# Q and K of a block in one input buffer, Q in the even partitions and K in the odd ones

## The chip, the cores and the metric

The kernel runs on one core of one Trainium2 chip. The metric is the device time of one execution in microseconds (us), median of several runs. A core has five engines that run side by side: TensorE (PE, matrix products), VectorE (DVE), ScalarE (ACT), GpSimd (POOL) and SyncE (SP). Sixteen DMA engines move data between the chip's memory (HBM) and the on-chip memory SBUF, which has 128 partitions. SP and ACT issue the transfers of this kernel, each through a queue of its own; the profile calls SP's data queue q1 and ACT's q10.

## The reference

```python
batch, n_heads, seq, head_dim = 8, 12, 1024, 64
def reference(q, k):
    return np.einsum('bhid,bhjd->bhij', q, k).astype(np.float32)
```

Each of the 8 x 12 = 96 heads is a product of a 1024 x 64 matrix Q with the transpose of a 1024 x 64 matrix K. Inputs and output are float32. The inputs are 2 x 25.2 MB, the output 402.7 MB.

## The kernel before

The 96 heads are worked in 11 blocks of 2, 2, 4, 8, 8 and then six times 12 heads (`sizes`). For each head, PE forms eight row tiles of 128 x 1024 scores (`scores`, L256): for each tile a weight load of Q (L317) and two products with 512 columns of K (L320), with a contraction over 64 partitions. ACT copies the scores from PSUM into one of three output buffers `o_sb` (L289), two tiles at a time, four copies per head; in the very first head DVE takes every second tile. After the last copy of a head, SP stores the whole buffer of 4 MB as one transfer (L305). A head may only be copied into an `o_sb` buffer when the store from three heads before has landed.

PE needs Q and K transposed (head_dim on partitions) and in half precision. For blocks 0 and 1 PE transposes (L244). For blocks 2 to 10 the way is:

- **Load** (L152 to L163). One transfer each for Q and K of the block brings the block's rows into 128 partitions, each partition a contiguous run of `R * D` floats with R = N * 1024 / 128 (24 KB for 12 heads). Q and K take turns in a ring of two buffers `x_sb`, so in practice one of them holds Q and the other K. Blocks 0 to 2 are loaded at the start into an output buffer that is still free, block 3 at the start into `x_sb`; all of these are SP's (and for single heads of K, ACT's). From block 4 on, ACT issues the loads, between its copies: `LOADS` (L81) tells after the second copy of which heads of block i the next load in the stream is issued; where no entry stands, it is heads 6 and 8. ACT waits there until all casts from that buffer are done.
- **Cast** (L201 to L220). POOL casts a chunk to half precision, four instructions of 32 partitions each, which also place the pieces for the transpose. A block of 12 heads has four chunks of 128 x 3072: Q in two parts, K in two parts. There are two buffers `half_sb` for them; block 2's chunks lie in unused ends of the operand buffers (`rooms`).
- **Transpose** (L222 to L236). DVE transposes a chunk in 32 x 32 squares into the operand buffers `qk_sb`, of which there are two sets, used by even and odd blocks. The first transpose of block i therefore waits until PE has finished block i - 2 (`over`).

Every engine works through its own list in order; the lists wait for one another only through counters. The transposes are written out beside the heads of the block before (`side` in `block`, L400), but DVE has nothing else to do after the start, so it runs them as soon as their casts and `over` allow. POOL, too, has only its list of casts.

Of the kernel before, what the change touches and what calls it, by code (L numbers as in the profile page):

```python
# [6 lines left out]
F16 = mybir.dt.float16  # L7
F32 = mybir.dt.float32
P = 128
# [50 lines left out]
def kernel(  # L60
# [6 lines left out]
    nc = tc.nc  # L67

    B, H, S, D = q.shape
# [8 lines left out]
    PE_BLOCKS, EARLY = 2, 3  # L78
    NMAX = max(sizes)
    CHUNK, HALVES = 96 * 32, 2  # L80
    LOADS = {0: (), 1: (), 2: (1, 3), 3: (4, 6), 4: (4, 6)}  # L81

    pool = ctx.enter_context(tc.tile_pool(name="sb", bufs=1))
    psum = ctx.enter_context(
        tc.tile_pool(name="ps", bufs=1, space=bass.MemoryType.PSUM)
    )
    ident = pool.tile([P, P], F16, tag="ident")
    x_sb = [pool.tile([P, NMAX * S * D // P], F32, name=f"x_sb{i}", tag=f"x{i}") for i in range(2)]
    half_sb = [pool.tile([P, CHUNK], F16, name=f"half{i}", tag=f"half{i}") for i in range(HALVES)]
    qk_sb = [  # L90
        [pool.tile([P, NMAX * S // 2], F16, name=f"{'qk'[x]}T{i}") for x in range(2)]
        for i in range(2)
    ]
    o_sb = [pool.tile([P, NT, S], F32, name=f"o_sb{i}", tag=f"out{i}") for i in range(3)]
# [10 lines left out]
    class Ring:  # L105
# [9 lines left out]
        def next(self):  # L115
# [4 lines left out]

    halves = Ring(half_sb)
    n, at = S * D // P * 2, 8 * S // 2
    rooms = Ring(
        [
            qk_sb[i][x][:, at + h * n : at + (h + 1) * n]
            for i in (1, 0)
            for x in range(2)
            for h in range(2)
        ]
    )  # L130
    inputs = Ring(x_sb)
    outs = Ring(o_sb)
    input_landing = {id(t): Landing(nc, f"x{i}_in") for i, t in enumerate(x_sb)}
    store_landing = {id(t): Landing(nc, f"out{i}_out") for i, t in enumerate(o_sb)}

    class Block:
        def __init__(self, i, first, N):
            self.i, self.first, self.N = i, first, N
            self.by_pe = i < PE_BLOCKS
            self.R = N * S // P  # L140
            self.elems = self.R * D
            self.cut = max(1, -(-self.R * 32 // CHUNK))
            self.raw = [None] * 2
            self.landed = [[] for _ in range(2)]
            self.raw_busy = [None] * 2
            self.rows = [None] * 2
            self.halves = {}
            self.qk = qk_sb[i % 2]
            self.ready = []
            self.over = []  # L150

        def load(self, x, eng, landing=None):  # L152
            events = []
            if self.raw[x] is None:
                buf, events, self.raw_busy[x] = inputs.next()
                self.raw[x] = buf[:, : self.elems]
                landing = input_landing[id(buf)]
            src = flat[x][self.first * S : (self.first + self.N) * S]
            eng.wait(events)
            dma = eng.eng.dma_start(  # L160
                out=self.raw[x], in_=src.rearrange("(p r) d -> p (r d)", p=P)
            )
            self.landed[x].append(landing.start(dma))  # L163

        def load_head(self, n, x, eng, landing):
            start = (self.first + n) * S
            m = S * D // P
            dma = eng.eng.dma_start(  # L168
                out=self.raw[x][:, n * m : (n + 1) * m],
                in_=flat[x][start : start + S].rearrange("(p r) d -> p (r d)", p=P),  # L170
            )
            self.landed[x].append(landing.start(dma))

        def cast_rows(self, x):
            n = S * D // P
            buf, events, busy = rooms.next()
            rows = buf[:, : 2 * n].rearrange("p (r h d) -> p r h d", h=2, d=D)
            for h in range(2):
                done = gps.run(
                    lambda: nc.gpsimd.tensor_copy(  # L180
                        out=rows[:, :, h],
                        in_=self.raw[x][:, h * n : (h + 1) * n].rearrange(
                            "p (r d) -> p r d", d=D
                        ),
                    ),
                    events + [self.landed[x][h]],
                )
            self.rows[x] = rows, done, busy
            if self.raw_busy[x] is not None:
                self.raw_busy[x].append(done)  # L190
            return done

        def chunks(self):
            return [
                (x, part, c)
                for x in range(2)
                for part in range(2)
                for c in range(self.cut)
            ]

        def cast_quads(self, x, part, c):  # L201
            m = self.R // self.cut
            buf, events, busy = (rooms if self.i == PE_BLOCKS else halves).next()
            dst = buf[:, : m * 32]
            raw = self.raw[x].rearrange("p (r h d) -> p r h d", h=2, d=32)
            for half in range(2):
                b = 2 * half + part
                for h in range(2):
                    q0 = 32 * (2 * half + h)
                    done = gps.run(  # L210
                        lambda: nc.gpsimd.tensor_copy(  # L211
                            out=dst[q0 : q0 + 32].rearrange("p (r d) -> p r d", d=32),
                            in_=raw[32 * b : 32 * b + 32, c * m : (c + 1) * m, h],
                        ),
                        events + self.landed[x],
                    )
            self.halves[x, part, c] = dst, done, busy
            if self.raw_busy[x] is not None:
                self.raw_busy[x][:] = [done]
            return done  # L220

        def transpose_quads(self, x, part, c):  # L222
            buf, cast, busy = self.halves.pop((x, part, c))
            n, m = self.N * S // 4, self.R // self.cut
            dst = self.qk[x][:, part * n : (part + 1) * n].rearrange(
                "c (i r) -> c r i", i=32
            )[:, c * m : (c + 1) * m]
            before = blocks[self.i - 2].over if self.i >= 2 else []
            done = dve.run(
                lambda: nc.vector.transpose(  # L230
                    out=dst, in_=buf.rearrange("p (r i) -> p r i", i=32)
                ),
                [cast] + before,
            )
            busy.append(done)
            self.ready.append(done)  # L236
# [103 lines left out]
    raw = early.rearrange("p t j -> p (t j)")  # L340
    at = 0
    for b in blocks[:EARLY]:
        for x in range(2):
            b.raw[x] = raw[:, at : at + b.elems]
            at += b.elems
        if b.by_pe:
            for n in range(b.N):
                for x in range(2):
                    b.load_head(n, x, (sp, act)[x], Landing(nc, f"e{b.i}{n}{x}"))
        else:  # L350
            for x in range(2):
                b.load(x, sp, Landing(nc, f"e{b.i}{x}"))
# [6 lines left out]
    def next_load(eng):  # L359
        if stream:  # L360
            b, x = stream.pop(0)
            assert b.i == EARLY or not any(i == b.i - 1 and c[0] == x for i, c in casts)
            b.load(x, eng)

    for x in range(2):
# [18 lines left out]
    def to_half(last):  # L384
        while casts:
            i, c = casts[0]
            if i > last or (blocks[i], c[0]) in stream:
                return
            if not (rooms if i == PE_BLOCKS else halves).free():
                return  # L390
            done = blocks[i].cast_quads(*c)
            if i == 2:
                early_busy[:] = [done]
            casts.pop(0)
# [5 lines left out]
    def block(i, heads, regions, w):  # L400
        b = blocks[i]
        nxt = blocks[i + 1] if i + 1 < len(blocks) else None
        for n in heads:
            side = {}
            if nxt and nxt.by_pe:
                if n == 1:
                    side = {
                        u: [
                            lambda x=u // 2: nxt.transpose_rows(
                                x, regions.next(), dve, nc.vector.tensor_copy  # L410
                            )
                        ]
                        for u in (1, 3)
                    }
            elif nxt:
                parts = nxt.chunks()
                some = [s for m, s in enumerate(parts) if m * b.N // len(parts) == n]
                side = {0: [lambda s=s: transposed(nxt, s) for s in some]}
            if n in LOADS.get(i, (6, 8)):
                side[1] = side.get(1, []) + [lambda: next_load(act)]  # L420
            b.scores(n, side, regions, w)
            to_half(i + 2 + (n == b.N - 1))
# [50 lines left out]
```

## Time and profile before

| what | value |
|---|---|
| median of 3 runs | 1062.28 us (1061.65 to 1062.32) |
| profiled execution | 1061.94 us |
| its span, first to last instruction | 1059.8 us |
| PE, ACT, DVE, POOL busy | 66%, 66%, 44%, 33% |
| moved by DMA | 453.19 MB, mean 428 GB/s |
| read from HBM, written to HBM | 50.33 MB, 402.65 MB |

The page of the profile has, for each engine, the time in which it executed instructions, the span in 40 equal slices (a digit is tenths of busy time; for DMA the mean over the 16 engines, and the GB/s that they moved), the DMA queues with packets and bytes and the share of the 16 engines' time that their packets took, a chain of work followed back from the last instruction, and groups of equal instructions by line. In a group, "x96 | 263.3, 2743 | 466.9 <-DMA ..." means 96 instructions, 263.3 us in total, 2743 ns each, and 466.9 us of idle time of that engine ahead of them, with what ended the idle time. For transfers the last number is the median time from issue to landing. A row of the view of waits names who waited, for whom, the total in us, how often and the longest wait. In the view of windows, a row gives a stretch of the span, its length, the busy time of PE, PE's weight loads, DVE, ACT and POOL with their instruction counts, the clock, the DMA share and the GB/s.

### The profile page before, as it was taken

What the parts mean: (1) busy time and instruction counts of PE and PEld (TensorE: products, weight loads), DVE (VectorE), ACT (ScalarE), POOL (GpSimd) and SP (SyncE); (2) the same over time, 40 slices, a digit from 0 to 9 for tenths busy, and PEclk for the clock granted to TensorE, in tenths of its full rate; (3) what the DMA queues carried; (4) which work ended last, traced back from release to release, by engine and by line L of the source; (5) the groups of instructions that cost most, each with busy time, mean ns of one, the idle gap of its engine ahead of it and who ended that gap; (6) DMA issues with size and microseconds to landing.
All of it is one profiled execution on the core that took longest, in us unless ns stands there. A gap on an engine that the chain in (4) does not pass through costs nothing.

```text
span 1059.8 us, 3258 instructions
## 1 busy us (share of the span) xinstructions
PE 700.6 (66%) x1568; PEld 127.2 (12%) x800; DVE 470.5 (44%) x43; ACT 697.5 (66%) x386; POOL 345.7 (33%) x158
## 2 busy tenths in 40 slices
PE   6875855675577557875577755778557777778770
PEld 2111100110011001110011100111001111111110
DVE  2998701991696006970069600696007960000000
ACT  4766755665677557785577755777557778777771
POOL 7667316445370340803407043070431700000000
DMA  9999999999999999999999999999999999999998
GB/s 391 433 432 420 436 423 424 435 427 426 435 430 430 427 431 433 433 425 427 433 435 434 423 424 433 432 434 425 426 433 432 434 435 432 434 434 429 433 433 357
DMA packets 17584, 453.19 MB, mean 428 GB/s; under 512 B 1953, under 2 KB 1953, under 8 KB 2977
## 3 DMA queue, kind: packets, MB, share of 16 engines
q1 hardware_dynamic: 14976, 410.00, 90.0%
q10 hardware_dynamic: 2592, 42.99, 9.7%
q8 instruction: 9, 0.15, 0.0%
q14 instruction: 7, 0.05, 0.0%
HBM read 50.33 MB, written 402.65 MB: 427 GB/s over the span
## 4 chain that ended last, share of the span: by engine, by line
DMA 71%; ACT 17%; PE 7%; DVE 1%; issue 1%; POOL 0%; ACTq 0%; SPq 0%
DMA out_dram<-o_sb 70%; ACT o_sb L289 17%; PE ps_all L320 7%; DVE qT L230 1%; DVE kT L230 0%; DMA o_sb<-in_q_dram 0%; PE ps_all L244 0%; POOL qT L180 0%; DVE kT L251 0%; ACT kT L251 0%; ACTq L36 0%; SPq L168 0%; SPq L468 0%; SPq L97 0%
## 5 line engine op out<-in xcount | busy, mean ns | idle before, releaser
L289 ACT COPY o_sb<-ps_all 128x2048 f32<-128x2048 f32 (+1 forms) x384 | 695.2, 1861 | 332.1 <-DMA out_dram<-o_sb 298.8
L320 PE MATMUL ps_all<-kT,qT 64*128 64x512 f16 x1536 | 696.5, 616 | 327.2 <-ACT o_sb L289 321.8
L211 POOL CAST half<-x_sb 32x3072 f16<-32x3072 f32 (+1 forms) x128 | 323.7, 2529 | 491.4 <-DMA x_sb<-in_q_dram 245.9
L230 DVE STREAM_TRANSPOSE qT<-half 128x3072 f16<-128x3072 f16 (+1 forms) x16 | 222.8, 14127 | 370.7 <-PE ps_all L320 368.9
L317 PEld LDWEIGHTS <-qT 64*128 64x128 f16 x768 | 124.1, 162 | 896.5 <-issue 889.0
L230 DVE STREAM_TRANSPOSE kT<-half 128x3072 f16<-128x3072 f16 (+1 forms) x16 | 224.2, 14219 | 3.4 <-POOL half L211 3.4
L230 DVE STREAM_TRANSPOSE kT<-kT 128x1024 f16<-128x1024 f16 x2 | 9.4, 4873 | 0.0
L230 DVE STREAM_TRANSPOSE qT<-qT 128x1024 f16<-128x1024 f16 x2 | 9.2, 4786 | 0.0
L211 POOL CAST qT<-o_sb 32x1024 f16<-32x1024 f32 x8 | 8.3, 1036 | 1.2 <-DMA o_sb<-in_q_dram 0.8
L211 POOL CAST kT<-o_sb 32x1024 f16<-32x1024 f32 x8 | 8.3, 1036 | 0.5
L251 DVE COPY qT<-ps_all 128x1024 f16<-128x1024 f16 x2 | 2.4, 1224 | 10.8 <-PE ps_all L244 10.8
L289 DVE COPY o_sb<-ps_all 128x1024 f32<-128x1024 f32 x4 | 4.9, 1225 | 4.4 <-PE ps_all L320 4.4
L244 PE MATMUL ps_all<-ident,qT 128*128 128x128 f16 x16 | 2.1, 311 | 6.5 <-POOL qT L180 6.4
L251 ACT COPY kT<-ps_all 128x1024 f16<-128x1024 f16 x1 | 1.0, 1013 | 4.6 <-PE ps_all L244 4.6
L180 POOL CAST qT<-o_sb 128x512 f16<-128x512 f32 x4 | 2.3, 613 | 3.5 <-DMA o_sb<-in_q_dram 3.5
L251 DVE COPY kT<-ps_all 128x1024 f16<-128x1024 f16 x1 | 1.2, 1225 | 4.3 <-PE ps_all L244 4.3
L251 ACT ACT_TABLE_LOAD x1 | 1.3, 1283 | 2.8 <-issue 2.8
L180 POOL CAST kT<-o_sb 128x512 f16<-128x512 f32 x4 | 2.3, 614 | 1.3 <-DMA o_sb<-in_q_dram 1.3
L244 PE MATMUL ps_all<-ident,kT 128*128 128x128 f16 x16 | 2.0, 306 | 0.7 <-ACT o_sb L289 0.7
L244 PEld LDWEIGHTS ps_all<-ident,qT 128*128 128x128 f16 x16 | 1.5, 141 | 6.8 <-POOL qT L180 6.8
L244 PEld LDWEIGHTS ps_all<-ident,kT 128*128 128x128 f16 x16 | 1.5, 138 | 3.3 <-POOL qT L211 1.6
L372 POOL TENSOR_SCALAR_AFFINE_SELECT ident<-ident 128x128 f16<-128x128 f16 x1 | 0.3, 295 | 0.2 <-POOL ident L368 0.2
(5 smaller groups left out, 0.6 us busy)
## 6 DMA issues: line engine op xcount, KB each, us to landing
out_dram<-o_sb SPq DMA_DIRECT2D x96, 4096.0 KB, 21.5
x_sb<-in_q_dram ACTq DMA_DIRECT2D x6, 3072.0 KB, 22.7
x_sb<-in_k_dram ACTq DMA_DIRECT2D x6, 3072.0 KB, 22.0
x_sb<-in_q_dram SPq DMA_DIRECT2D x1, 2048.0 KB, 15.5
x_sb<-in_k_dram SPq DMA_DIRECT2D x1, 2048.0 KB, 20.9
x_sb<-in_q_dram ACTq DMA_DIRECT2D x1, 2048.0 KB, 19.2
x_sb<-in_k_dram ACTq DMA_DIRECT2D x1, 2048.0 KB, 20.2
o_sb<-in_k_dram ACTq DMA_DIRECT2D x4, 256.0 KB, 4.9
```

The costliest lines, as they stand in the source:

```text
L180: lambda: nc.gpsimd.tensor_copy(out=rows[:, :, h], in_=self.raw[x][:, h * n : (h + 1) * n].rearrange("p (r d) -> p r d", d=D),),
L211: lambda: nc.gpsimd.tensor_copy(out=dst[q0 : q0 + 32].rearrange("p (r d) -> p r d", d=32), in_=raw[32 * b : 32 * b + 32, c * m : (c + 1) * ...
L230: lambda: nc.vector.transpose(out=dst, in_=buf.rearrange("p (r i) -> p r i", i=32)),
L244: lambda: nc.tensor.transpose(t_ps[:, t], rows[:, t], ident),
L251: lambda: copy(out=dst, in_=t_ps.rearrange("c t m -> c m t")), [done]
L289: lambda: (nc.vector.tensor_copy if by_dve else nc.scalar.copy)(out=dst, in_=ps[:, : w * S]),
L317: return nc.tensor.ldweights(stationary, tile_position=(at, 0))
L320: return nc.tensor.add_instruction(mybir.InstMatmult(name=nc.get_next_instruction_name(), ins=[nc.tensor.lower_ap(moving), nc.tensor.lower ...
L372: lambda: nc.gpsimd.affine_select(out=ident, in_=ident, compare_op=mybir.AluOpType.not_equal, fill=1.0, base=0, pattern=[[-1, P]], channel ...
```

## The change

There is now one input buffer `x_sb` of 128 partitions and twice the length, as much memory as the two before. A block's rows of Q are cut into 64 runs instead of 128, each twice as long (48 KB for 12 heads), which go to partitions 0, 2, 4, ...; those of K go to partitions 1, 3, 5, ... Each load is still one transfer, now with 64 partitions in steps of two. This holds for blocks 2 to 10; the loads of single heads for blocks 0 and 1 keep their form.

A chunk for POOL and DVE then has Q and K together. A block of 12 heads still has four chunks of 128 x 3072 (`chunks`: two parts by two cuts), 8-head blocks four of 128 x 2048, and block 2 two of 128 x 2048 instead of four of 128 x 1024. The casts wait for both loads of the block. The transpose writes to Q's and K's operand buffer by turns, since they are now two halves of one tile, 12288 bytes apart.

Since Q and K share the buffer, a load of the next block waits until all casts of the block before are done, and `LOADS` is set anew: block 4's loads are issued in head 3 of block 2 and head 0 of block 3, block 5's in heads 6 and 7 of block 3, block 6's in head 7 of block 4 and head 0 of block 5, block 7's in heads 8 and 10 of block 5, and those of blocks 8 to 10 in heads 6 and 8 of the block two before. The transposes of the next block are written out beside heads 1 to N - 1 instead of 0 to N - 1. The buffers for block 2's chunks and for blocks 0 and 1 are two separate rings.

```diff
-    LOADS = {0: (), 1: (), 2: (1, 3), 3: (4, 6), 4: (4, 6)}
+    LOADS = {0: (), 1: (), 2: (3,), 3: (0, 6, 7), 4: (7,), 5: (0, 8, 10)}
...
-    x_sb = [pool.tile([P, NMAX * S * D // P], F32, name=f"x_sb{i}", tag=f"x{i}") for i in range(2)]
+    x_sb = pool.tile([P, NMAX * S * D // (P // 2)], F32, tag="x")
...
-        [pool.tile([P, NMAX * S // 2], F16, name=f"{'qk'[x]}T{i}") for x in range(2)]
+        pool.tile([P, 2, NMAX * S // 2], F16, name=f"qkT{i}", tag=f"qkT{i}")
...
-            self.R = N * S // P
+            self.R = N * S // (P // 2)
...
-            eng.wait(events)
+            eng.wait(self.free)
             dma = eng.eng.dma_start(
-                out=self.raw[x], in_=src.rearrange("(p r) d -> p (r d)", p=P)
-            )
-            self.landed[x].append(landing.start(dma))
+                out=self.raw[x::2], in_=src.rearrange("(a r) d -> a (r d)", a=P // 2)
+            )
+            self.landed[x].append((landing or input_landing[x]).start(dma))
...
         def chunks(self):
-            return [
-                (x, part, c)
-                for x in range(2)
-                for part in range(2)
-                for c in range(self.cut)
-            ]
+            return [(part, c) for part in range(2) for c in range(self.cut)]
...
-                        events + self.landed[x],
+                        events + self.landed[0] + self.landed[1],
...
-            n, m = self.N * S // 4, self.R // self.cut
-            dst = self.qk[x][:, part * n : (part + 1) * n].rearrange(
-                "c (i r) -> c r i", i=32
-            )[:, c * m : (c + 1) * m]
+            n, m = self.N * S // 2, self.R // self.cut
+            dst = qk_sb[self.i % 2][:, :, :n].rearrange(
+                "c x (t a r) -> c t r a x", t=2, r=self.R
+            )[:, part, c * m : (c + 1) * m]
             before = blocks[self.i - 2].over if self.i >= 2 else []
             done = dve.run(
                 lambda: nc.vector.transpose(
-                    out=dst, in_=buf.rearrange("p (r i) -> p r i", i=32)
+                    out=dst, in_=buf.rearrange("p (r a x) -> p r a x", a=16, x=2)
                 ),
...
-                some = [s for m, s in enumerate(parts) if m * b.N // len(parts) == n]
+                some = [s for m, s in enumerate(parts) if 1 + m * (b.N - 1) // len(parts) == n]
```

More of the change, by code (lines that the diff above doesn't have):

```diff
@@ L122 @@
     n, at = S * D // P * 2, 8 * S // 2
[L123 to L126, printed above, removed]
-            for x in range(2)
-            for h in range(2)
-        ]
-    )
-    inputs = Ring(x_sb)
+    unused = [[qk_sb[i][:, x, at:] for x in range(2)] for i in range(2)]
+    row_rooms = Ring([r[:, h * n : (h + 1) * n] for r in unused[1] for h in range(2)])
+    rooms = Ring(unused[0])
+    inputs = Ring([x_sb])
     outs = Ring(o_sb)
-    input_landing = {id(t): Landing(nc, f"x{i}_in") for i, t in enumerate(x_sb)}
+    input_landing = [Landing(nc, f"x{x}_in") for x in range(2)]
     store_landing = {id(t): Landing(nc, f"out{i}_out") for i, t in enumerate(o_sb)}
@@ L139, in __init__ @@
             self.by_pe = i < PE_BLOCKS
-            self.R = N * S // P
+            self.R = N * S // (P // 2)
             self.elems = self.R * D
             self.cut = max(1, -(-self.R * 32 // CHUNK))
-            self.raw = [None] * 2
+            self.raw = None
+            self.free = []
             self.landed = [[] for _ in range(2)]
-            self.raw_busy = [None] * 2
+            self.raw_busy = None
             self.rows = [None] * 2
             self.halves = {}
-            self.qk = qk_sb[i % 2]
+            self.qk = [qk_sb[i % 2][:, x] for x in range(2)]
             self.ready = []
@@ L152, in load @@
         def load(self, x, eng, landing=None):
[L153 to L157, printed above, removed]
+            if self.raw is None:
+                buf, self.free, self.raw_busy = inputs.next()
+                self.raw = buf[:, : self.elems]
             src = flat[x][self.first * S : (self.first + self.N) * S]
-            eng.wait(events)
+            eng.wait(self.free)
             dma = eng.eng.dma_start(
-                out=self.raw[x], in_=src.rearrange("(p r) d -> p (r d)", p=P)
+                out=self.raw[x::2], in_=src.rearrange("(a r) d -> a (r d)", a=P // 2)
             )
-            self.landed[x].append(landing.start(dma))
+            self.landed[x].append((landing or input_landing[x]).start(dma))
         def load_head(self, n, x, eng, landing):
@@ L168, in load_head @@
             dma = eng.eng.dma_start(
-                out=self.raw[x][:, n * m : (n + 1) * m],
+                out=self.raw[:, (x * self.N + n) * m : (x * self.N + n + 1) * m],
                 in_=flat[x][start : start + S].rearrange("(p r) d -> p (r d)", p=P),
@@ L175, in cast_rows @@
             n = S * D // P
-            buf, events, busy = rooms.next()
+            buf, events, busy = row_rooms.next()
             rows = buf[:, : 2 * n].rearrange("p (r h d) -> p r h d", h=2, d=D)
@@ L181, in cast_rows @@
                         out=rows[:, :, h],
-                        in_=self.raw[x][:, h * n : (h + 1) * n].rearrange(
-                            "p (r d) -> p r d", d=D
-                        ),
+                        in_=self.raw[
+                            :, (x * self.N + h) * n : (x * self.N + h + 1) * n
+                        ].rearrange("p (r d) -> p r d", d=D),
                     ),
@@ L188, in cast_rows, with cast_quads @@
             self.rows[x] = rows, done, busy
-            if self.raw_busy[x] is not None:
-                self.raw_busy[x].append(done)
             return done
         def chunks(self):
-            return [
-                (x, part, c)
-                for x in range(2)
-                for part in range(2)
-                for c in range(self.cut)
-            ]
-        def cast_quads(self, x, part, c):
+            return [(part, c) for part in range(2) for c in range(self.cut)]
+        def cast_quads(self, part, c):
             m = self.R // self.cut
@@ L204, in cast_quads @@
             dst = buf[:, : m * 32]
-            raw = self.raw[x].rearrange("p (r h d) -> p r h d", h=2, d=32)
+            raw = self.raw.rearrange("p (r h d) -> p r h d", h=2, d=32)
             for half in range(2):
@@ L214, in cast_quads, with transpose_quads @@
                         ),
-                        events + self.landed[x],
+                        events + self.landed[0] + self.landed[1],
                     )
-            self.halves[x, part, c] = dst, done, busy
-            if self.raw_busy[x] is not None:
-                self.raw_busy[x][:] = [done]
-            return done
-        def transpose_quads(self, x, part, c):
-            buf, cast, busy = self.halves.pop((x, part, c))
-            n, m = self.N * S // 4, self.R // self.cut
-            dst = self.qk[x][:, part * n : (part + 1) * n].rearrange(
-                "c (i r) -> c r i", i=32
-            )[:, c * m : (c + 1) * m]
+            self.halves[part, c] = dst, done, busy
+            if self.raw_busy is not None:
+                self.raw_busy[:] = [done]
+            return done
+        def transpose_quads(self, part, c):
+            buf, cast, busy = self.halves.pop((part, c))
+            n, m = self.N * S // 2, self.R // self.cut
+            dst = qk_sb[self.i % 2][:, :, :n].rearrange(
+                "c x (t a r) -> c t r a x", t=2, r=self.R
+            )[:, part, c * m : (c + 1) * m]
             before = blocks[self.i - 2].over if self.i >= 2 else []
@@ L342 @@
     for b in blocks[:EARLY]:
-        for x in range(2):
-            b.raw[x] = raw[:, at : at + b.elems]
-            at += b.elems
+        b.raw = raw[:, at : at + b.elems]
+        at += b.elems
         if b.by_pe:
@@ L361, in next_load @@
             b, x = stream.pop(0)
-            assert b.i == EARLY or not any(i == b.i - 1 and c[0] == x for i, c in casts)
+            assert b.i == EARLY or not any(i == b.i - 1 for i, c in casts)
             b.load(x, eng)
@@ L386, in to_half @@
             i, c = casts[0]
-            if i > last or (blocks[i], c[0]) in stream:
+            if i > last or any((blocks[i], x) in stream for x in range(2)):
                 return
```

## The prediction

> **What bounds the kernel now.** The first view is the page: the busy slices and the DMA rate, then the queues.
>
> ```profile
> span 1059.8 us, 3258 instructions
> ...
> DMA  9999999999999999999999999999999999999998
> GB/s 391 433 432 420 436 423 424 435 427 426 435 430 430 427 431 433 433 425 427 433 435 434 423 424 433 432 434 425 426 433 432 434 435 432 434 434 429 433 433 357
> DMA packets 17584, 453.19 MB, mean 428 GB/s; under 512 B 1953, under 2 KB 1953, under 8 KB 2977
> ...
> q1 hardware_dynamic: 14976, 410.00, 90.0%
> q10 hardware_dynamic: 2592, 42.99, 9.7%
> ```
>
> The DMA row is full from the first slice to the last, and the two data queues together take 90.0 + 9.7 = 99.7% of the 16 engines' time. No compute engine is above 66%. So the bytes set the time: 453.19 MB, at no slice above 436 GB/s. Nothing on PE, ACT, DVE or POOL costs anything until it makes the store queue run dry. The change moves the same bytes, so what it does to the time is what it does to the rate of the loads, unless it makes a block's operands late.
>
> The second view is the chain that ended last and the waits; the third, the landing times.
>
> ```profile
> DMA 71%; ACT 17%; PE 7%; DVE 1%; issue 1%; POOL 0%; ACTq 0%; SPq 0%
> ```
> ```profile
> DVE qT L230 <- PE ps_all L320: 368.9, 6, 72.7
> PE ps_all L320 <- ACT o_sb L289: 321.8, 187, 8.0
> ACT o_sb L289 <- DMA out_dram<-o_sb: 298.8, 88, 8.0
> ```
> ```profile
> out_dram<-o_sb SPq DMA_DIRECT2D x96, 4096.0 KB, 21.5
> x_sb<-in_q_dram ACTq DMA_DIRECT2D x6, 3072.0 KB, 22.7
> x_sb<-in_k_dram ACTq DMA_DIRECT2D x6, 3072.0 KB, 22.0
> ```
>
> ACT waits for a store to land before 88 of 96 heads, PE waits for ACT, DVE waits for PE: everyone waits for the stores. A store of 4.19 MB is about 9.7 us of DMA work (4.19 MB / 433 GB/s), and lands 21.5 us after its issue: its own 9.7, about 9.7 of the store ahead of it, and some 2 of latency. So when a store is issued one whole store still lies ahead of it: a head may come about 9.7 us late before the DMA engines idle.
>
> **The loads.** Count packets: 96 stores, 8 loads of single heads, 4 loads by SP and 14 by ACT are 122 transfers; 122 x 128 rows + 122 x 16 = 17568, which is 14976 + 2592. So one row is one packet, each transfer has 16 more small ones, one for each engine, and all transfers are now spread over 16 engines with 8 rows each. 18 loads change form (blocks 2 to 10, Q and K): 64 rows of twice the length, 4 to an engine, 18 x 64 = 1152 packets fewer. Their bytes are 2 x 1.05 + 4 x 2.10 + 12 x 3.15 = 48.2 MB. The ACT queue is the row for their price: 9.7% of 1059.8 us is 102.8 us for 42.99 MB, 2.39 us/MB. They take 48.2 x 2.39 = 115 us now.
>
> What a load into every second partition costs is in no row: every transfer here has 128 rows on neighbouring partitions. **Bounds:** the nearest row, the present load, gives no cost; from below, all loads at the store queue's rate (410.00 MB in 90.0%, 430 GB/s instead of 418) would win 48.2/0.418 - 48.2/0.430 = 3 us. The upper end is that two engines come to the same part of SBUF and share what one gets: then each row takes twice as long, +115 us. That such a share exists is an inference from this: loads and stores run within 3% of each other (418 and 430), though one reads HBM and the other writes it, so what limits both is more likely an engine or its way into SBUF than HBM. [...] Four rows in steps of two span eight partitions, so the 16 engines no longer divide SBUF as before, and at equal steps they would meet in pairs.
>
> I take the meeting case, at the rate at which two engines are in a load together. An engine with both queues waiting takes a packet of each in turn. Loads of 48 KB rows beside stores of 32 KB rows: it is in a load 48/80 = 0.6 of that stretch, so its partner meets it 0.6 of its load time. With 32 KB rows: 0.5. At the start, loads alone: 1.
> - blocks 2 and 3 (6.3 MB, 15.0 us, no stores yet): +15.0
> - block 4 (4.2 MB, 10.0 us): +5.0
> - blocks 5 to 10 (37.7 MB, 90.2 us): +54.1
>
> Sum +74 us. The profiled execution took 1061.94 us, its span 1059.8, and the median of the runs is 1062.28, 0.3 above it: 1061.94 + 74 = 1136.
>
> [...]
>
> **The other edits, beside the DMA.**
>
> ```profile
> L211 POOL CAST half<-x_sb 32x3072 f16<-32x3072 f32 x96 | 263.3, 2743 | 466.9 <-DMA x_sb<-in_q_dram 241.4 <-DVE qT L230 220.8
> L230 DVE STREAM_TRANSPOSE kT<-half 128x3072 f16<-128x3072 f16 x12 | 186.9, 15785 | 0.0
> L230 DVE STREAM_TRANSPOSE kT<-half 128x2048 f16<-128x2048 f16 x4 | 37.3, 9523 | 3.4 <-POOL half L211 3.4
> L230 DVE STREAM_TRANSPOSE kT<-kT 128x1024 f16<-128x1024 f16 x2 | 9.4, 4873 | 0.0
> ```
> Casts and transposes of blocks 3 to 10 keep number and size. Block 2 has 8 casts of 2048 (about 1.89 us by the 2048 row) for 16 of 1.036: 15.1 instead of 16.6 us, and 2 transposes for 4: 19.0 instead of 18.6 us. Block 2's casts now wait for Q and K: K lands about 14.4 us (issue 3.31 + 11.1), so they run 14.4 to 29.5, ending where they did (29.4). Head 4 waits for the transposes as before; 0.4 us later is hidden by the two stores then queued.
>
> The transposes write in another order: two elements 12288 B apart, then 384 B on, where before every step was 192 B. Present rows: 4.76 ns an element at 64 B steps, 4.65 at 128, 5.14 at 192. I take 15.7 us, the row of the same size; ends: 14.3 (4.65 ns) and twice, 31.4.
>
> The single buffer ties each load to all casts of the block before it, and the casts to both loads. On ACT's queue the loads stand behind copies, and copies behind loads that wait. Tightest is block 5: K is issued in block 3's last head, about 179.7 us (PE finishes that head at 181.6), lands 22 later at 202; casts of 11.0 and transposes of 15.7 alternate: first transpose 213, last ends 213 + 4 x 15.7 = 276.
>
> ```profile
> 273.58 30.93 DVE L230 STREAM_TRANSPOSE qT<-half 128x3072 f16<-128x3072 f16 x2 [30.25 <-PE ps_all L320]
> ```
> ```profile
> 280.41 3.64 ACT L289 COPY o_sb<-ps_all 128x2048 f32<-128x2048 f32 x2 [4.96 <-DMA out_dram<-o_sb]
> ```
> Block 4 ends at 273.6 (the DVE row starts on it), and ACT's first copy of block 5 starts at 280.4, on a landing. PE may start some 1.9 us before that, at 278.5: 276 is in time, with the 9.7 us of queued store behind. Before, it was ready at 243; this cover shrinks from 35 us to 2.5 + 9.7. Block 4, by the same steps, is ready at 160 for 181.6, block 6 at 380 for 407.9. ACT's waits on the casts (block 5's end at 255, the next load is due at 270) are over when it comes to them. Cost: nothing.
>
> **Rivals.**
> 1. *Loads keep their rate.* For it: all 16 engines still get equal bytes. Then 1062. Chance 0.20.
> 2. *Faster.* Windows with loads run below those without:
> ```profile
> 240.00:262.00 22.00, 13.40 (x30) 2.42 (x15) 3.32 (x1) 14.55 (x8) 12.14 (x5) 1.00 1.00 427
> 300.00:340.00 40.00, 29.05 (x64) 5.16 (x32) 35.24 (x3) 30.37 (x17) 11.38 (x5) 1.00 1.00 433
> ```
> (last column GB/s.) 6 of 433 over 22 us is 0.3 us a load, 18 loads 5.5 us; if half as many packets alternating with the stores won half of it, 1059. It decides from 2.1 us on. Against it: a packet that is twice as long keeps the engine as long. Chance 0.15.
> 3. *The transposes get slow at the new steps.* At twice the time block 5 is ready at 213 + 126 = 339, against 278.5 + 9.7: 50 us of idle DMA, 1112; later blocks (126 of 134 us) keep up. It begins to cost above (288.2 - 213)/4 = 18.8 us each, 20% more. Against it: steps of 64 to 192 B differ by 10%. Chance 0.08.
>
> **How the numbers follow.** The meeting of loads has 0.57, with a range of its own from 1085 (a third of the sum) to 1177 (all of the 115 us). 0.2% of the median, 2.1 us, is what a measurement of this kernel can tell from no change: faster 0.15 (rival 2), same 0.20 (rival 1), slower 0.57 + 0.08 = 0.65. The range 1060 to 1165 leaves out most of rival 2 (0.13) and the top of the forecast (0.06).
>
> **What would show it.** Packets 17584 - 1152 = 16432. Right: the ACT queue's share grows from 9.7% to about 15% for the same 42.99 MB, the GB/s row falls well below 420 in slices with loads and not in others, and ACT's wait for out_dram grows while the DMA row stays full. Wrong if that share stays near 9.7% (rivals 1 and 2, told apart by the GB/s of load slices), or if the DMA row itself drops around 276 to 340 us with PE waiting for DVE (rival 3).

## The result, and the profile after

The changed kernel takes 1071.49 us (median of 5 runs, 1069.60 to 1074.56) against 1062.28 us: a ratio of 1.0092, 95% interval 1.0071 to 1.0113. It is slower, by 9.2 us, where 74 us were forecast. Its own runs lie 5 us apart, those of the kernel before 1.4 us. The profiled execution took 1069.60 us, the fastest of the five, with a span of 1067.8 us: 8.0 us more than the span before.

From the page of the changed kernel, the DMA rows, the queues and the landing times:

```profile
span 1067.8 us, 3241 instructions
...
DMA  9999999999999999999999999999999999999996
GB/s 393 431 426 419 434 430 423 432 432 430 428 431 431 424 429 433 435 431 423 425 431 433 424 419 417 435 433 421 422 423 432 433 433 433 433 432 433 431 431 286
DMA packets 16431, 453.19 MB, mean 424 GB/s; under 512 B 1952, under 2 KB 1952, under 8 KB 2976
...
q1 hardware_dynamic: 14720, 410.00, 89.3%
q10 hardware_dynamic: 1696, 42.99, 10.0%
...
out_dram<-o_sb SPq DMA_DIRECT2D x96, 4096.0 KB, 21.5
x_sb<-in_q_dram ACTq DMA_DIRECT2D x6, 3072.0 KB, 19.5
x_sb<-in_k_dram ACTq DMA_DIRECT2D x6, 3072.0 KB, 18.9
x_sb<-in_q_dram SPq DMA_DIRECT2D x1, 2048.0 KB, 14.1
x_sb<-in_k_dram SPq DMA_DIRECT2D x1, 2048.0 KB, 18.3
```

The packets are as counted ahead (16431 for 16432). But the ACT queue's share is 10.0%, not the 15% of the forecast: 10.0% of 1067.8 is 106.8 us for the same 42.99 MB, 4.0 us more than the 102.8 before. The lowest slices in the middle are 417 to 424 GB/s, hardly below the 420 to 427 before. The last slice stands out: 286 instead of 357. The view of windows over the last 12 us of the span says it more exactly. Its columns are the stretch, its length, busy time of PE, weight loads, DVE, ACT and POOL, the clock, the DMA share and GB/s. Before:

```profile
1047.80:1059.80 12.00, 0.00 (x0) 0.00 (x0) 0.00 (x0) 0.00 (x0) 0.00 (x0) 1.00 0.63 273
```
After:
```profile
1055.80:1067.80 12.00, 0.00 (x0) 0.00 (x0) 0.00 (x0) 0.00 (x0) 0.00 (x0) 1.00 0.25 107
```

The 16 engines are busy for 63% of these 12 us before and for 25% after: 12 x 0.38 = 4.6 us more in which an average engine has finished and another has not. These shares are rounded. Summed over the packet records of the traces and divided by 16, all packets took 1057.8 us before and 1060.6 after, 2.8 more. The rest of the span, in which an average engine moves nothing, grew from 2.0 to 7.2 us, 5.2 more. So the 8.0 us between the two profiled executions have two parts: longer packets, and engines that end at different times. The first part comes from the loads: by the same records, the packets of ACT's queue took 103.3 us before and 106.7 after. The DMA records of the trace show the second part directly. Each transfer has 16 packets of 4 B (1952 for 122 transfers, in both kernels), one for each engine by the count. Here are the five latest of the 16 at the end of three stores, in us after the median one, worked out from those packets:

```
store   before                       after
  25    0.6  1.8  2.5  2.8  3.3      0.7  1.0  3.4  4.0  4.0
  61    0.6  1.0  1.5  2.5  2.5      1.1  2.4  3.1  6.8  7.1
  93    1.4  2.2  2.5  2.7  2.8      0.7  0.7  2.9  7.3  7.6
```

In this execution of the changed kernel two engines fall behind while there are loads, 7.1 us by store 61, and hardly further after it (7.6 us at store 93), when two loads are left. Each store is cut over all 16 engines and has landed when the last of its 16 small packets has (each is counted as landed 0.35 us after its end, the median in both traces), so the slowest engine sets the end. The first experiment below shows that engines can also fall behind without the changed loads.

The compute engines are not the cause. The waits of the changed kernel:

```profile
POOL half L198 <- DMA x_sb<-in_k_dram: 409.3, 7, 72.4
PE ps_all L307 <- ACT o_sb L276: 325.1, 186, 12.0
ACT o_sb L276 <- DMA out_dram<-o_sb: 308.6, 88, 12.0
...
PE ps_all L307 <- DVE qkT L217: 7.7, 2, 4.6
```

ACT still waits for a store before 88 heads, 308.6 us instead of 298.8. PE waited for a transpose twice, 7.7 us in all. The longer wait, 4.6 us at block 3's start, lies in a stretch (60 to 90 us) with a DMA share of 1.00.

### The profile page after: what moved, and what is told of

The parts are those of the page before. It is cut to its first block, busy times and chain, and to the rows that moved or that the text cites. A ratio compares the mean times of both kernels' runs of the same rounds, so it can differ in the third digit from the quotient of the medians.

```text
span 1067.8 us, 3241 instructions
## 1 busy us (share of the span) xinstructions
PE 700.6 (66%) x1568; PEld 127.4 (12%) x800; DVE 426.6 (40%) x41; ACT 697.2 (65%) x386; POOL 343.8 (32%) x150
## 2 busy tenths in 40 slices
DMA packets 16431, 453.19 MB, mean 424 GB/s; under 512 B 1952, under 2 KB 1952, under 8 KB 2976
## 3 DMA queue, kind: packets, MB, share of 16 engines
q10 hardware_dynamic: 1696, 42.99, 10.0%
## 4 chain that ended last, share of the span: by engine, by line
DMA 71%; ACT 17%; PE 7%; DVE 2%; issue 1%; POOL 0%; ACTq 0%; SPq 0%
DMA out_dram<-o_sb 71%; ACT o_sb L276 17%; PE ps_all L307 7%; DVE qkT L217 2%; DMA o_sb<-in_q_dram 0%; PE ps_all L231 0%; POOL qkT L174 0%; DVE qkT L238 0%; ACT qkT L238 0%; ACTq L36 0%; SPq L162 0%; SPq L454 0%; SPq L97 0%
## 5 line engine op out<-in xcount | busy, mean ns | idle before, releaser
L276 ACT COPY o_sb<-ps_all 128x2048 f32<-128x2048 f32 (+1 forms) x384 | 694.9, 1859 | 340.3 <-DMA out_dram<-o_sb 308.6
L307 PE MATMUL ps_all<-qkT 64*128 64x512 f16 x1536 | 696.5, 617 | 335.2 <-ACT o_sb L276 325.1
L217 DVE STREAM_TRANSPOSE qkT<-half 128x3072 f16<-128x3072 f16 (+1 forms) x32 | 400.3, 12798 | 418.4 <-POOL half L198 239.5
L304 PEld LDWEIGHTS <-qkT 64*128 64x128 f16 x768 | 124.3, 162 | 904.2 <-issue 890.9
L217 DVE STREAM_TRANSPOSE qkT<-qkT 128x2048 f16<-128x2048 f16 x2 | 18.3, 9334 | 0.0
L198 POOL CAST qkT<-o_sb 32x2048 f16<-32x2048 f32 x8 | 15.1, 1887 | 3.6 <-DMA o_sb<-in_k_dram 3.2
L238 DVE COPY qkT<-ps_all 128x1024 f16<-128x1024 f16 x3 | 3.7, 1225 | 15.2 <-PE ps_all L231 15.2
L231 PE MATMUL ps_all<-ident,qkT 128*128 128x128 f16 x32 | 4.1, 307 | 7.3 <-POOL qkT L174 6.5
L174 POOL CAST qkT<-o_sb 128x512 f16<-128x512 f32 x8 | 4.6, 613 | 3.9 <-DMA o_sb<-in_q_dram 3.9
L231 PEld LDWEIGHTS ps_all<-ident,qkT 128*128 128x128 f16 x32 | 3.1, 138 | 10.1 <-POOL qkT L174 6.8
## 6 DMA issues: line engine op xcount, KB each, us to landing
x_sb<-in_q_dram SPq DMA_DIRECT2D x1, 2048.0 KB, 14.1
x_sb<-in_k_dram SPq DMA_DIRECT2D x1, 2048.0 KB, 18.3
x_sb<-in_k_dram ACTq DMA_DIRECT2D x1, 2048.0 KB, 14.7
```

The lines of the kernel that those rows point to most:

```text
L174: lambda: nc.gpsimd.tensor_copy(out=rows[:, :, h], in_=self.raw[:, (x * self.N + h) * n : (x * self.N + h + 1) * n].rearrange("p (r d) -> ...
L198: lambda: nc.gpsimd.tensor_copy(out=dst[q0 : q0 + 32].rearrange("p (r d) -> p r d", d=32), in_=raw[32 * b : 32 * b + 32, c * m : (c + 1) * ...
L217: lambda: nc.vector.transpose(out=dst, in_=buf.rearrange("p (r a x) -> p r a x", a=16, x=2)),
L231: lambda: nc.tensor.transpose(t_ps[:, t], rows[:, t], ident),
L238: lambda: copy(out=dst, in_=t_ps.rearrange("c t m -> c m t")), [done]
L276: lambda: (nc.vector.tensor_copy if by_dve else nc.scalar.copy)(out=dst, in_=ps[:, : w * S]),
```

## The experiments

The theory after the result: the form of the loads costs the time, not the schedule; and it is rows in steps of two partitions that cost, by some meeting in SBUF. Rivals: the schedule (one buffer, later loads), the length of the packets, and HBM.

**Loads of 128 rows in the one buffer**

```diff
+            e = self.elems // 2
...
-                out=self.raw[x::2], in_=src.rearrange("(a r) d -> a (r d)", a=P // 2)
+                out=self.raw[:, x * e : (x + 1) * e],
+                in_=src.rearrange("(p r) d -> p (r d)", p=P),
```

> The changed kernel with one edit: each load again fills 128 neighbouring partitions (rows of 24 KB for 12 heads), Q in the first half of the one buffer and K in the second. One buffer, casts, transposes and load places stay as changed. The casts then mix Q and K, so the scores are not those of the reference; the work and the waits are the same. Theory of the loads' form (stepped partitions or long rows cost 9 us): back to 1061 to 1063 us, last slice of the GB/s row about 350. Rival, the schedule (one buffer, later loads, both landings for each cast): stays at 1069 to 1074.

1062.95 us, ratio to the kernel before 1.0008 (1.0000 to 1.0017). One buffer, later loads, casts that wait for both landings and the new transposes cost 0.5 us, at most some 2: the schedule rival falls. The other 8.5 us are the form of the loads.

The last slice was expected back at about 350 GB/s, and that did not happen. The profiled execution, the slowest of twelve (1065.75 us), ends like that of the changed kernel:

```profile
GB/s 394 433 424 423 434 431 432 432 432 424 430 429 431 433 428 433 432 429 429 437 433 434 419 432 430 434 431 426 428 439 432 432 433 432 432 433 426 434 430 276
1051.90:1063.90 12.00, 0.00 (x0) 0.00 (x0) 0.00 (x0) 0.00 (x0) 0.00 (x0) 1.00 0.21 90
```

At the end of store 93 its five latest engines are 2.8, 5.1, 5.2, 8.4 and 8.5 us behind the median. Its packets took 1056.7 us, and the rest of the span is 7.3 us, as much as in the changed kernel (7.2). So engines also fall behind with loads of 128 rows, at least in one execution. That the steps make them do so in this kernel is not shown. What separates the two profiled executions, 1067.8 and 1063.9 us of span, is the packet time, 3.9 us. The other 4.6 of the 8.5 us between the medians cannot be placed: the profiled execution was the fastest of the changed kernel and the slowest of this run.

**Steps, with rows of half the length**

```diff
...
+            for h in range(2):
+                dma = eng.eng.dma_start(
+                    out=self.raw[x::2, h * e : (h + 1) * e],
+                    in_=src[:, h * e : (h + 1) * e],
+                )
...
```

> The changed kernel with each stepped load cut into two transfers of half the row length (64 partitions in steps of two, rows of 24 KB for 12 heads), issued one behind the other. Theory of the steps (engines meet in SBUF beside stores): still 1069 to 1074, since the partitions are the same. Rival, the length of the packets (a 48 KB packet lets an engine fall behind by twice as much): back to 1061 to 1064.

1068.33 us, 1.0056 (1.0043 to 1.0069): neither. With packets as short as before, steps still cost 5.4 us over the 1062.95 of the 128 rows; the long packet adds 3.2. In the profiled execution the packets took 1061.5 us and the rest of the span is 3.4 us: against the kernel before, most of its cost is packet time.

**One long load of 128 rows**

```diff
+            if x == 1:
+                self.landed[1] = self.landed[0]
+                return
+            src = flat[0][first * S : (first + 2 * self.N) * S]
+            dma = eng.eng.dma_start(
+                out=self.raw, in_=src.rearrange("(p r) d -> p (r d)", p=P)
+            )
```

> The changed kernel with one load for both tensors of a block into 128 neighbouring partitions, rows of 48 KB for 12 heads, twice as many bytes in one transfer, all of them from Q; the load of K is left out, so the scores are not those of the reference. Length without steps. Theory that a long packet alone sets engines apart: 1066 to 1072. Rival, the steps are needed for it: 1062 to 1064.

1061.07 us, 0.9984 (0.9975 to 0.9994): below both ranges. 48 KB packets into 128 neighbouring partitions cost nothing here; length added time only with the steps (3.2 us, from 1068.33 to 1071.49).

**Q in the lower, K in the upper half of the partitions**

```diff
-                out=self.raw[x::2], in_=...
+                out=self.raw[64 * x : 64 * x + 64], in_=...
```

> The changed kernel with Q in partitions 0 to 63 and K in 64 to 127 instead of even and odd ones; row length, packets and schedule as changed. The casts then mix Q and K, so the scores are not those of the reference. Theory of meeting in SBUF: neighbouring halves are the worst case, the upper bound of the prediction: up to 1177 us, at least 1100. Rival, only the length of the rows counts: 1069 to 1074 as for the steps.

1154.37 us, 1.0870 (1.0856 to 1.0884), as the theory had it. Only the partitions differ from the changed kernel, so loads can hinder one another by where they write in SBUF. The 92 us lie between the prediction's sum (74) and its upper end (115). The queues in the page of this run, 14.7% of 1154.7 us = 169.7 us for the loads that took 102.8 before:

```profile
q1 hardware_dynamic: 14720, 410.00, 84.5%
q10 hardware_dynamic: 1696, 42.99, 14.7%
```

**Transfers alone, first bench**

```
for stores in (0, 5):
    for form in ("rows128", "steps", "contig"):
        SP: issue `stores` stores of 4.19 MB;  ACT: issue 6 loads of 3.15 MB in this form
        both wait until all have landed
```

> Transfers alone, no scores are computed: six stages, each of six loads of 3.15 MB on ACT's queue; first the three forms with no stores (128 rows; 64 rows in steps of two, even and odd by turns; 64 neighbouring rows, low and high half by turns), then the same three, each beside five stores of 4.19 MB on SP's queue. At the rate of the page (about 430 GB/s) a stage takes 44 us plus some 3 without stores and 93 plus 3 with them. Theory of meeting in SBUF: steps are slower than 128 rows, without stores by up to twice, and neighbouring halves take about 88 us. Rival, rows' length beside stores: all three equal without stores; with stores both 64-row forms some us longer than 128 rows. Third, nothing of this: all equal in both.

Each bench is one execution. The view of windows, one row for each stage (length, POOL, clock, DMA share, GB/s):

```profile
7.90:54.40 46.50, 0.00 (x0) 1.00 0.96 406
54.40:101.40 47.00, 0.00 (x0) 1.00 0.94 402
101.40:195.00 93.60, 0.00 (x0) 1.00 0.97 202
195.00:290.20 95.20, 0.00 (x0) 1.00 0.98 419
290.20:386.80 96.60, 0.00 (x0) 1.00 0.98 412
386.80:522.90 136.10, 0.00 (x0) 1.00 0.96 293
```

Alone, 64 rows in steps of two are as fast as 128 rows (47.0 and 46.5 us), and 64 neighbouring rows take twice as long (93.6). Beside stores the steps cost 1.4 us in six loads, in a single stage. The neighbouring halves cost 40.9 us beside stores (136.1 against 95.2), nearly the 47.1 that they cost alone; by the prediction's share of 0.6 it would have been about 28, an estimate. "Steps meet each other" falls; what is left is something that they meet only beside stores.

**Loads in the stores' queue**, in the changed kernel and in the kernel before:

```diff
-                side[1] = side.get(1, []) + [lambda: next_load(act)]
+                side[1] = side.get(1, []) + [lambda: next_load(sp)]
```

> The changed kernel with the loads from block 4 on issued by SP instead of ACT, at the same heads: they then stand in one queue with the stores, and an engine does a load's packets in one go instead of by turns with a store's. Theory of the mixture (stepped rows cost something only by turns with stores): 1061 to 1065. Rival, the stepped rows cost the same wherever they stand: 1069 to 1074.

> The kernel before with the same edit: loads from block 4 on issued by SP. Theory of the mixture: its load windows (420 to 427 GB/s) come up to the 430 to 435 of the others, 1057 to 1061. Rival: nothing changes, 1061 to 1063.

1064.12 us (1.0015, 1.0006 to 1.0023) with steps, 1064.45 us (1.0017, 1.0009 to 1.0026) with 128 rows. The form of the load no longer makes a difference, so in these runs the steps cost something only when their queue is not that of the stores. The packet records fit the theory that packets come by turns from two queues and in one go from one. They name no engine, but a packet can be linked to the one that starts within a few ns of its end: so linked, an estimate, a 24 KB packet of a load is followed by one of the stores' queue in 1341 of 1535 cases in the kernel before. And the 128 packets of a 12-head load start within 15.3 to 16.6 us in the kernel before, and within 9.8 to 13.7 us when the loads stand in the stores' queue. The hope for the kernel before was wrong: it got 0.17% slower. Its loads land later, too, since they stand behind stores (Q 29.4 us instead of 22.7).

**Transfers alone, second bench: one load at a time beside stores**

```
for turn in range(2):
    for form in ("rows128", "steps", "split", "long128"):
        SP: issue 22 stores;  ACT: 37.7 MB of loads, each issued when the one before has landed
        both wait until all have landed
```

> Transfers alone, no scores are computed: eight stages, four forms twice over, each with 22 stores of 4.19 MB queued by SP and 37.7 MB of loads by ACT, each load issued when the one before it has landed: 128 rows; 64 rows in steps of two; the same in two transfers of half the length; 128 rows of 48 KB. At 432 GB/s a stage takes 301 us plus some 3. Theory from the first runs: 128 rows 304, steps 3 to 7 us longer, halves between them, long rows of 128 partitions near 128 rows; the second turn gives the same order. Rival: all within 1 us of each other, and the cost needs the rest of the kernel.

```profile
7.90:315.80 307.90, 0.00 (x0) 1.00 0.99 422
315.80:628.60 312.80, 0.00 (x0) 1.00 0.98 416
628.60:941.10 312.50, 0.00 (x0) 1.00 0.99 416
941.10:1247.30 306.20, 0.00 (x0) 1.00 0.99 425
1247.30:1556.90 309.60, 0.00 (x0) 1.00 0.99 420
1556.90:1870.20 313.30, 0.00 (x0) 1.00 0.98 415
1870.20:2181.60 311.40, 0.00 (x0) 1.00 0.99 418
2181.60:2489.30 307.70, 0.00 (x0) 1.00 0.99 423
```

The rows are 128 rows, steps, halves of steps, long 128 rows, and the same again. Steps cost 4.9 and 3.7 us per 12 loads without any compute engine, halves 4.6 and 1.8, long rows -1.7 and -1.9. The order is that of the kernels; the same form differs by up to 1.7 us between the turns. The packet records tell what the cost consists of. With steps the packets took 305.7 and 306.4 us, hardly more than with 128 rows (304.9 and 305.0), and the rest of the stage, in which engines have ended and wait for the last, is 7.1 and 6.9 us instead of 3.0 and 4.6. With halves the packets took longer, 309.5 and 309.0 us, and the rest is 3.0 and 2.4. So here the long stepped rows do set engines apart.

**Partitions 32 to 95**

```diff
...
+            if self.i <= EARLY:
+                dst = self.raw[x::2]
+            else:
+                dst = self.raw[32:96]
+                eng.wait([x_clear])
+                if x == 1:
+                    eng.wait([self.landed[0][-1]])
```

> The changed kernel, but from block 4 on each load goes to the 64 neighbouring partitions 32 to 95 (rows of 48 KB as changed; K's load waits for Q's and overwrites it, the other partitions keep old values, so the scores are not those of the reference; DVE first clears the unused end of the buffer). [...] Theory of crossing into another engine's part: 1061 to 1065. Rival, 64 rows cost beside stores wherever they go: 1069 to 1074.

1065.13 us, 1.0022 (1.0012 to 1.0033). 64 rows of the same length, from the same places in HBM, in neighbouring partitions across the middle: 6.4 of the 9.2 us are gone, 2.6 stay. That is just above the range of the theory and far below the rival's. The theory was that a load costs time where an engine writes it into partitions from which another engine reads stores, and that 32 to 95 avoid this. Both are the author's assumption; no run shows which engine reaches which partitions.

**Transfers alone, third bench: beside stores and beside copies within HBM**

```
for form, beside in (rows128, stores), (steps, stores), (32 to 95, stores), (rows128, HBM copies), (steps, HBM copies):
    SP: 22 transfers of 4.19 MB, from SBUF or from HBM, to HBM;  ACT: 12 loads as in the second bench
```

> Transfers alone as in the bench before, 12 loads and 22 transfers of 4.19 MB on the other queue in each stage, twice over: 128 rows, steps and partitions 32 to 95 beside stores from SBUF; then 128 rows and steps beside copies of the same size within HBM, which touch no SBUF. Theory of crossing into another engine's part of SBUF: 308, 313, 308 beside stores, and beside copies within HBM steps within 1 us of 128 rows. Rival, it is the reading of 64 long rows from HBM beside other traffic: partitions 32 to 95 at 313 as well, and steps some 4 us above 128 rows beside copies too.

```profile
7.90:314.40 306.50, 0.00 (x0) 1.00 1.00 424
314.40:626.90 312.50, 0.00 (x0) 1.00 0.98 416
626.90:937.20 310.30, 0.00 (x0) 1.00 0.99 419
937.20:1290.20 353.00, 0.00 (x0) 1.00 0.99 368
1290.20:1636.10 345.90, 0.00 (x0) 1.00 0.99 376
1636.10:1942.00 305.90, 0.00 (x0) 1.00 1.00 425
1942.00:2257.20 315.20, 0.00 (x0) 1.00 0.97 413
2257.20:2568.20 311.00, 0.00 (x0) 1.00 0.98 418
2568.20:2921.60 353.40, 0.00 (x0) 1.00 0.98 368
2921.60:3270.70 349.10, 0.00 (x0) 1.00 0.98 372
```

Beside stores, steps cost 6.0 and 9.3 us, partitions 32 to 95 3.8 and 5.1. With steps the rest of the stage, while engines wait for the last, is again longer: 6.1 and 8.9 us, against 1.4 and 1.4 with 128 rows. Beside copies that read HBM instead of SBUF, steps are 7.1 and 4.3 us *faster* than 128 rows; "within 1 us" was wrong, and so was the rival. That fits a cost that needs a neighbour that reads SBUF, but does not show it: these stages run at 368 to 376 GB/s instead of 413 to 425, so something else may bound them and hide a few us. Against the reading of long rows from HBM as the cause speaks that partitions 32 to 95 read the same rows and cost less. That they cost over half of the steps in this bench, and a quarter in the kernel, was not expected. If an engine's crossing into partitions that another engine reads is the cause, it is not the whole of it; no run shows the crossing itself.

**The loads of a block together**, in the kernel before, because the one long load had been 0.2% faster than it:

```diff
-    LOADS = {0: (), 1: (), 2: (1, 3), 3: (4, 6), 4: (4, 6)}
+    LOADS = {0: (), 1: (), 2: (3,), 3: (6,), 4: (6,)}
...
-            if n in LOADS.get(i, (6, 8)):
-                side[1] = side.get(1, []) + [lambda: next_load(act)]
+            if n in LOADS.get(i, (8,)):
+                side[1] = side.get(1, []) + [lambda: next_load(act)] * 2
```

> The kernel before with the two loads of a block issued one right behind the other, after the second copy of head 8 (head 6 in blocks 3 and 4, head 3 in block 2), instead of two heads apart. The run with one load per block of 128 rows of 48 KB came out 0.2% below the kernel before. Theory that each start of a load beside stores costs some tenths of a us: half as many starts, 1060 to 1061.5. Rival, the gain there came from the longer rows: 1062 to 1063.5.

1063.01 us, 1.0007 (0.9998 to 1.0016): no gain. The edit halves the places at which loads are issued; the transfers are as many as before, so the price of a start is not tested by it. No version that computes the scores came out faster than the kernel before.

## Why the prediction was wrong in size

**What bounds the kernel**: right. DMA stays full until the last slice (39 slices at 9 tenths or more, the last at 6), and compute stays hidden (PE, the busiest engine, 700.6 of 1067.8 us).

**"I take the meeting case"** is the step that failed. The prediction let two loads meet, and loads in steps of two do not slow each other: alone they take 47.0 us against 46.5. The steps do cost, but beside stores of another queue, and far less: 8.5 us between the medians of the changed kernel and of the run with 128 rows, 3.9 us of packet time between their profiled executions. So "slower" came out in part by luck, since the reason given for it did not occur. The prediction's own sign of being wrong, an ACT queue near 9.7%, came true with 10.0%. Twice the time, the price put on a meeting, came in one form, neighbouring halves alone (93.6 against 46.5 us); that two engines meet there is not shown. Term by term:

- *Blocks 2 and 3, +15.0*: nothing. In the kernel these loads landed earlier than before, in 14.1 and 18.3 us; before, in its page:
```profile
x_sb<-in_q_dram SPq DMA_DIRECT2D x1, 2048.0 KB, 15.5
x_sb<-in_k_dram SPq DMA_DIRECT2D x1, 2048.0 KB, 20.9
```
- *Block 4, +5.0, and blocks 5 to 10, +54.1, by the share of time in a load*: the engine time of ACT's queue grew by 4.0 us by the rounded shares, 3.4 by the packet records. That share priced a meeting of two loads, which does not occur.
- *Not in the sum*: that engines fall behind one another and are waited for at the end, 5.2 us between the profiled executions. The run with 128 rows shows it too, so how much of it belongs to the change is open; in the benches it came with the long stepped rows (6.1 to 8.9 us a stage, against 1.4 to 4.6).

The inference "Four rows in steps of two span eight partitions, so the 16 engines no longer divide SBUF as before, and at equal steps they would meet in pairs" assumed which engine moves which row, and that the engines divide SBUF among them. No view shows the engine of a packet, no run shows such a division, and the guess about the pairs was wrong or does not matter at this rate.

What the runs show is the rate of each form: alone, 64 neighbouring partitions got half of what 128 rows got (202 against 406 GB/s), and 64 in steps of two nearly all of it (402 GB/s). A store reads SBUF and a load writes it; no run shows where the two could meet, so whether they contend there stays open.

**The numbers that follow**: two are slightly off. A third of the sum puts the lower end of the forecast at 1087, not 1085. And since the 15.0 us of blocks 2 and 3 fall on SP's queue, the sum means 14% for ACT's queue, not 15%.

**The other edits at no cost**: right, by the run with 128 rows (+0.5 us). Within them, two sizes were off. The transposes of 3072 took 13.9 us, not 15.7 (the lower end was 14.3), and block 5 was ready at 252 us (197.9 + 54.4), not 276:

```profile
197.90 54.41 DVE L217 STREAM_TRANSPOSE qkT<-half 128x3072 f16<-128x3072 f16 x4 [50.69 <-POOL half L198]
```

**Rivals**: the transposes did not get slow. "Faster" had its mechanism half right: half as many long packets came with 0.16% less in the run with one load of 128 rows. That run also has half as many loads, so which of the two won is not shown. "Loads keep their rate" holds for loads alone and in the stores' queue.

Not settled: where between a stepped load and a store the cost arises, in SBUF or elsewhere; which engine carries which row; why partitions 32 to 95 still cost something; and why engines stay behind, in one execution with 128 rows too.

## What to carry to other kernels

A transfer that is free by itself may cost beside another one (steps: 0.5 us more in six loads alone, 3.7 to 9.3 us more in twelve, one at a time, beside stores): measure a new load form next to the traffic that it will run with, in the same queues. When bytes bound a kernel, look at the last microseconds, too: the mean rate in the middle hides that some of the 16 engines fall behind, and the DMA share of the last 12 us (0.63 to 0.25 here) shows it. One execution does not tell where it comes from: the old form of load had 0.21 in one. Give a load all 128 partitions when stores run beside it in another queue (1062.95 against 1071.49 us here); packet length alone cost nothing here (1061.07 us).

## What was not expected of the hardware

- Transposes on DVE that write elements 12288 B and 384 B apart are faster than those with steps of 192 B: 13.9 against 15.7 us for 128x3072.
- Moving all loads into the stores' queue, with 128 rows, made the kernel before 0.17% slower, though the loads then no longer share the engines with a second queue.
- Beside copies within HBM, 64 long rows in steps were 4 to 7 us faster per stage than 128 rows (345.9 and 349.1 against 353.0 and 353.4).
- The time of 128 rows in the one buffer spread from 1062.07 to 1065.75 us over 12 runs; its profiled execution was the slowest of them and ended with two engines some 8.5 us behind.
